# Experts with 96 slots: a weight's chunks first all in one tile shape, then in the other, and the scatter behind the next transposes

## Chip, cores and metric

The kernel runs on one core of a Trainium2 chip. The metric is the device time of one launch in microseconds (us); the text compares medians of several runs, and the profile comes from one execution.

## What is computed

Two decoder layers for 256 tokens of width 1024 (float32). Each layer has a token mixer (SSD, latent attention and a gated unit side by side) and a channel mixer with modulation, residual and layer norm around it. The channel mixer of the second layer is a mixture of 8 experts, and the change lies in it alone:

```python
combine = jnp.sum(jax.nn.one_hot(top_i, N_EXPERTS) * gates[..., None], axis=-2)
for e in range(N_EXPERTS):
    out = out + combine[..., e:e + 1] * swiglu(h, w1[e], w3[e], w2[e])   # silu(h w1) * (h w3), times w2
```

Each token takes two experts. w1 and w3 are 1024 x 2816, w2 is 2816 x 1024.

## The kernel before, in words

The experts are worked off one after the other in 8 places, place 0 to place 7. A place has a fixed number of slots for tokens, `CAPS = [96, 64, 128, 64, 96, 64, 96, 64]`; which expert comes to which place is sorted at run time, and a general loop at the end (`overflow`, skipped here) takes what doesn't fit.

For each place `gather` picks its tokens by matmuls with a one-hot matrix `hot` and transposes them into `st.t`. The hidden width is worked off in three blocks of 1024, 1024 and 768 columns (`BLOCKS = [8, 8, 6]`). `stage1(place, s)` multiplies the tokens by a block of w1 and then of w3 and forms silu(a) * g in `sa`. `turn` transposes `sa`: matmuls with the identity on TensorE (L1093 and L1101; L1086 for 128 slots) into PSUM, from where ScalarE or VectorE copies them. `stage2` multiplies by the block's rows of w2 into `st.po`, which collects all three blocks. After the third block `scatter` copies `po` out of PSUM (L1160, or L1184 and L1185), spreads the rows over the 256 tokens by matmuls with `hott` (L1165, or L1190 and L1191), and VectorE adds them to `yacc` (L1169, L1196). The loop runs stage1 of a block ahead of stage2 of the block before it; in the text, a weight is one block of w1, w3 or w2.

Weights come from DRAM in chunks: `moe_chunk` (L1005) on SP's queue, 280 of them, 35 for each place. A weight of stage1 has four chunks, one of stage2 four, four or three. A chunk lies in one of 11 buffers, taken in turn (6 of `ring`, 5 of `ring2`), and a transfer into a buffer starts when the last instruction that reads the chunk in it is done.

The shape of the matmuls depends on the slots. The stationary operand is the tokens. With 64 slots it has 64 columns, and two matmuls stand side by side in the array (the `wide` shape: L1029 in stage1, L1120 in stage2; 8 records for a chunk). With 96 slots the first 64 go through `wide` and the other 32 through `slim`, four matmuls of 32 columns side by side (L1037 and L1127; 16 records for a chunk, 12 in stage1 of the third block). Both read every chunk. With 128 slots the weights are split into two parts on ScalarE and VectorE (L146, L148) and multiplied by full-width matmuls (L153 to L155).

In the code a weight of a 96-slot place is taken in pairs of chunks: wide 0, wide 1, slim 0, slim 1, then slim 2, slim 3, wide 2, wide 3. The last chunk of a weight with three is slim 2, wide 2.

PSUM buffers come from two pools of four: `acp` (`act_t`: `po`, the transposes, the scatter's and gather's products) and the pool of stage1's sums.

Instructions are not issued in the order of the code. The tile framework fixes each engine's order when the program is built: at each step of its own clock it takes the earliest instruction of the code whose operands it holds to be ready. So a wide pass whose chunk it believes to be still under way is overtaken by a slim pass on a chunk that is there. On the chip the order is then fixed.

Of the kernel before, what the change touches and what calls it, by code (L numbers as in the profile page):

```python
# [52 lines left out]
def tile_decoder(ctx: ExitStack, tc: tile.TileContext, x_in, c_t, c_in, cst, prm, rows, lnrows, gateb, ada, w_in, w_out,  # L53
# [856 lines left out]
    def moe_mixer(x, ad, rs, mp, ring2):  # L910
# [11 lines left out]
        def gather(place):  # L922
            st = state[place] = Ada()
            cap = st.cap = CAPS[place]
            sl, pos = chosen(place, "sl"), chosen(place, "pos")

            hot = mp.tile([P, 2, P], F, tag="hot", name=nm("hot"), bufs=2)
            for i in range(2):
                to, slots = hot[:, i, 0:cap], iota[:, 0:cap]
                if cap == 64:  # L930
                    to = hot[:, i, :].rearrange("p (a s) -> p a s", a=2)
                    slots = iota[:, None, 0:64].to_broadcast([P, 2, 64])
                ins = (pool if place else dve).tensor_scalar(to, slots, pos[:, i, :], sl[:, i, :], op0=OP.is_equal, op1=OP.mult).ins
                if place == 0:
                    mark["hot"] = ins
            st.t = mp.tile([P, KD, P], F, tag="xt", name=nm("xt"), bufs=2)
            scb, shb = ad.sc[:, :, None], ad.sh[:, :, None]

            def put(rows, nq, groups, of, wid):

                g = mp.tile([P, 512], F, tag="gtmp", name=nm("gtmp"))
                act.activation(g[0:rows, 0:nq * P], of[0:rows, 0:nq * P], AF.Copy)
                pt = act_t([P, nq, rows])
                for q in range(nq):
                    pe.transpose(pt[:, q, :], g[0:rows, q * P:q * P + P], ident[0:rows, 0:rows])
                ks, c0 = wid
                pv = pt.rearrange("p q (g s) -> p g q s", g=groups)
                w = rows // groups
                shape = [P, groups, nq, w]
                to = st.t[:, ks, c0:c0 + w].rearrange("p (g q) s -> p g q s", g=groups)  # L950
                bc = [v[:, ks, :].rearrange("p (g q) o -> p g q o", g=groups).to_broadcast(shape) for v in (scb, shb)]
                dve.tensor_tensor(to, pv, bc[0], op=OP.mult)
                dve.tensor_tensor(to, to, bc[1], op=OP.add)

            if cap == P:
                for c in range(2):
                    ps = act_t([P, 512])
                    for i in range(2):
                        pe.matmul(ps, hot[:, i, :], x[:, i, 512 * c:512 * c + 512], start=(i == 0), stop=(i == 1))
                    put(P, 4, 1, ps, (slice(4 * c, 4 * c + 4), 0))  # L960
                st.th = mp.tile([P, KD, P], FR, tag="xhi", name=nm("xth"))
                st.tl = mp.tile([P, KD, P], FR, tag="xlo", name=nm("xtl"))
                for c in range(2):
                    ks = slice(4 * c, 4 * c + 4)
                    act.activation(st.th[:, ks, :], st.t[:, ks, :], AF.Copy)
                    dve.tensor_tensor(st.tl[:, ks, :], st.t[:, ks, :], f32(st.th)[:, ks, :], op=OP.subtract)
            else:
                ps = act_t([P, 512])
                for i in range(2):
                    for c in range(2):  # L970
                        pe.matmul(ps[64 * c:64 * c + 64, :], hot[:, i, 0:64], x[:, i, 512 * c:512 * c + 512],
                                  start=(i == 0), stop=(i == 1), tile_position=(0, 64 * c))
                put(P, 4, 2, ps, (slice(0, KD), 0))
                if cap == 96:
                    ps = act_t([P, 256])
                    for i in range(2):
                        for g in range(4):
                            pe.matmul(ps[32 * g:32 * g + 32, :], hot[:, i, 64:96], x[:, i, 256 * g:256 * g + 256],
                                      start=(i == 0), stop=(i == 1), tile_position=(0, 32 * g))
                    put(P, 2, 4, ps, (slice(0, KD), 64))  # L980
            rows = P if cap == 64 else cap
            st.hott = mp.tile([P, T], F if cap == 64 else FR, tag="hott", name=nm("hott"), bufs=3)
            pt = act_t([P, T])
            for i in range(2):
                pe.transpose(pt[0:rows, i * P:i * P + P], hot[:, i, 0:rows], ident)
            act.activation(st.hott[0:rows, :], pt[0:rows, :], AF.Copy)
# [10 lines left out]
        def moe_chunk(place, n, width=2048):  # L997
# [7 lines left out]
            sp.dma_start(t[:, 0:width], src[:, 0:width])  # L1005
            return t


        def stage1(place, s):
            st = state[place]  # L1010
# [5 lines left out]
            for wsel in range(2):  # L1016
                if st.cap == P:
                    ps = [mmt([P, half]) for _ in range(2)]
                else:
                    ps = mmt([P, half])  # L1020
                    p3 = mmt([P, 256]) if st.cap == 96 else None
                ws = []

                def wide(j):
                    w = ws[j]
                    for k1 in range(2):
                        k = 2 * j + k1
                        for c in range(2):
                            pe.matmul(ps[64 * c:64 * c + 64, :], st.t[:, k, 0:64], w[:, k1, half * c:half * c + half],  # L1029
                                      start=(k == 0), stop=(k == KD - 1), tile_position=(0, 64 * c))  # L1030

                def slim(j):
                    w = ws[j]
                    for k1 in range(2):
                        k = 2 * j + k1
                        for g in range(ng):
                            pe.matmul(p3[32 * g:32 * g + 32, :], st.t[:, k, 64:96], w[:, k1, 256 * g:256 * g + 256],  # L1037
                                      start=(k == 0), stop=(k == KD - 1), tile_position=(0, 32 * g))

                for j in range(4):  # L1040
                    w = moe_chunk(place, 12 * s + 4 * wsel + j, 2 * wd)[:, 0:2 * wd].rearrange("p (k c) -> p k c", k=2)
                    ws.append(w)
                    if st.cap == P:
                        for k1 in range(2):
                            k = 2 * j + k1
                            with ExitStack() as late:
                                if place == 0 and s == 0 and wsel == 0 and k >= EARLY:
                                    late.enter_context(tc.issue_after(mark["hot"]))
                                wh, wl = moe_split(w[:, k1, :], [P, wd])
                            for c in range(2):  # L1050
                                cs = slice(half * c, half * c + half)
                                mm3(ps[c], (st.th[:, k, :], st.tl[:, k, :]), (wh[:, cs], wl[:, cs]), k == 0, k == KD - 1)
                    elif st.cap == 64:
                        wide(j)
                    elif j % 2:
                        for f, jj in ((wide, j - 1), (wide, j), (slim, j - 1), (slim, j)) if j == 1 else (
                                (slim, j - 1), (slim, j), (wide, j - 1), (wide, j)):
                            f(jj)
                out.append(ps if st.cap == P else [ps, p3])
            pa_, pg_ = out  # L1060
            if st.cap == P:
# [44 lines left out]
        def stage2(place, s, th, tl):  # L1106
# [23 lines left out]
            for m in range(nq):  # L1130
                w = moe_chunk(place, 12 * s + 8 + m).rearrange("p (k c) -> p k c", k=2)
                ws.append(w)
                if st.cap == P:
                    whl = [moe_split(w[:, u, :], [P, D]) for u in range(2)]
                    for u, hf in ((0, 0), (0, 1), (1, 0), (1, 1)):
                        wh, wl = whl[u]
                        t = 2 * m + u
                        hs = slice(512 * hf, 512 * hf + 512)
                        mm3(po[hf], (th[:, t, :], tl[:, t, :]), (wh[:, hs], wl[:, hs]), first(t), last(t))
                elif st.cap == 64:  # L1140
                    wide(m)
                elif m % 2 or m == nq - 1:
                    ms = [m - 1, m] if m % 2 else [m]
                    for f in ((wide, slim) if m == 1 else (slim, wide)):
                        for mm in ms:
                            f(mm)

        def scatter(place):
            st = state[place]
# [147 lines left out]
        for place in range(NE):  # L1297
            for s in range(3):
# [4 lines left out]
                sa = stage1(place, s)  # L1303
                if prev is not None:
                    stage2(*prev)
                    if prev[1] == 2:
                        scatter(prev[0])
                prev = (place, s, *turn(place, s, sa))
        stage2(*prev)
        scatter(prev[0])  # L1310
        overflow()
# [210 lines left out]
```

## Time and profile before

| | |
|---|---|
| median of 3 runs | 1257.72 us (1256.67 to 1258.25) |
| the profiled execution | 1257.42 us, its span 1255.6 us |
| TensorE busy | 1170.9 us, 93% of the span |
| VectorE, ScalarE busy | 506.3 us (40%), 384.3 us (31%) |
| experts (stage1 of place 0 to the last stage2) | about 550 us to 1236 us of the span |

Times in rows are microseconds from the span's start. PE is TensorE's matmuls, PEld its loads of the stationary operand, DVE VectorE, ACT ScalarE, POOL GpSimd, SP the queue that issues transfers. A busy TensorE is not TensorE at its peak, since matmuls overlap and their ends are modelled; the starts are what is compared below.

### The profile page before, as it was taken

What the parts mean: (1) busy time and instruction counts of PE and PEld (TensorE: products, weight loads), DVE (VectorE), ACT (ScalarE), POOL (GpSimd) and SP (SyncE); (2) the same over time, 40 slices, a digit from 0 to 9 for tenths busy, and PEclk for the clock granted to TensorE, in tenths of its full rate; (3) what the DMA queues carried; (4) which work ended last, traced back from release to release, by engine and by line L of the source; (5) the groups of instructions that cost most, each with busy time, mean ns of one, the idle gap of its engine ahead of it and who ended that gap; (6) DMA issues with size and microseconds to landing.
All of it is one profiled execution on the core that took longest, in us unless ns stands there. A gap on an engine that the chain in (4) does not pass through costs nothing. (4 is left out here: it accounts for less than half of the span.)

```text
span 1255.6 us, 18705 instructions
## 1 busy us (share of the span) xinstructions
PE 1170.9 (93%) x7667; PEld 704.4 (56%) x7667; DVE 506.3 (40%) x815; ACT 384.3 (31%) x558; POOL 54.5 (4%) x58
## 2 busy tenths in 40 slices
PE   5999979999997999879999999899999999999994
PEld 2877758999986976534433557743334333333331
DVE  2776465777557754521003477630010020300214
ACT  1776435444444754210002457620010010100100
POOL 0100100000000000010000002200000000000001
PEclk9999889999998997989999999999999999999997
DMA  9957646788554475638999999999999999999994
GB/s 378 386 200 295 219 167 227 279 299 332 171 192 167 163 288 198 252 157 312 350 426 408 426 424 367 364 395 349 425 423 371 423 391 426 412 401 375 413 423 163
DMA packets 59592, 402.97 MB, mean 321 GB/s; under 512 B 6751, under 2 KB 7143, under 8 KB 17390
## 3 DMA queue, kind: packets, MB, share of 16 engines
q1 hardware_dynamic: 59358, 401.47, 81.3%
q8 instruction: 62, 1.02, 0.3%
q10 hardware_dynamic: 144, 0.26, 0.1%
q14 instruction: 28, 0.23, 0.0%
HBM read 399.61 MB, written 2.10 MB: 320 GB/s over the span
## 5 line engine op out<-in xcount | busy, mean ns | idle before, releaser
L1029 PE MATMUL mm<-w,xt 128*64 128x512 f32 (+1 forms) x1344 | 288.7, 561 | 0.0
L148 DVE TENSOR_TENSOR wlo<-w,whi 128x1024 fp32r<-128x1024 f32 (+1 forms) x180 | 220.0, 1229 | 111.9 <-ACT whi L146 110.0
L146 ACT ACTIVATE whi<-w 128x1024 fp32r<-128x1024 f32 (+1 forms) x188 | 194.1, 1041 | 177.8 <-PE mm L154 87.8
L1029 PEld LDWEIGHTS mm<-w,xt 128*64 128x64 f32 x1344 | 94.4, 137 | 165.0 <-issue 163.7
L153 PE MATMUL mm<-hhi,whi 128*128 128x256 f32 x608 | 175.5, 290 | 4.8 <-ACT hhi L348 4.8
L154 PE MATMUL mm<-hlo,whi 128*128 128x256 f32 x608 | 174.8, 288 | 0.8 <-DVE hlo L349 0.8
L155 PE MATMUL mm<-hhi,wlo 128*128 128x256 f32 x608 | 173.7, 286 | 0.0
L1072 DVE TENSOR_TENSOR sa<-mm,sa 128x512 f32<-128x512 f32 (+3 forms) x30 | 17.4, 580 | 371.9 <-PE mm L1029 193.0
L1120 PE MATMUL acc<-w,ht 128*64 128x512 f32 x616 | 146.5, 597 | 0.0
L153 PEld LDWEIGHTS mm<-hhi,whi 128*128 128x128 f32 x608 | 118.6, 195 | 9.5 <-ACT hhi L348 6.0
L154 PEld LDWEIGHTS mm<-hlo,whi 128*128 128x128 f32 x608 | 118.6, 195 | 2.4 <-DVE hlo L349 1.8
L155 PEld LDWEIGHTS mm<-hhi,wlo 128*128 128x128 f32 x608 | 118.4, 195 | 0.6 <-issue 0.5
L1120 PEld LDWEIGHTS acc<-w,ht 128*64 128x64 f32 x616 | 43.6, 137 | 81.8 <-issue 80.7
L1071 ACT ACTIVATE sa<-mm 128x512 f32<-128x512 f32 (+3 forms) x30 | 15.2, 507 | 202.6 <-PE mm L1029 116.0
L1095 ACT ACTIVATE ht<-acc 128x512 f32<-128x512 f32 (+1 forms) x21 | 11.8, 561 | 199.2 <-PE acc L1093 199.2
L1037 PE MATMUL mm<-w,xt 128*32 128x256 f32 x1056 | 70.2, 382 | 0.0
L1037 PEld LDWEIGHTS mm<-w,xt 128*32 128x32 f32 x1056 | 34.1, 109 | 44.8 <-issue 24.6
L200 PE MATMUL mm<-w,cs_rep 128*32 128x512 f32 x304 | 41.1, 654 | 9.6 <-DMA w<-in_ada_dram 9.1
L154 PE MATMUL mm<-wlo,xth 128*128 128x512 f32 (+1 forms) x96 | 36.7, 382 | 1.6 <-POOL wlo L148 1.6
L155 PE MATMUL mm<-whi,xtl 128*128 128x512 f32 (+1 forms) x96 | 36.1, 376 | 0.0
L280 POOL TENSOR_TENSOR rs<-rs,mhalf 128x1 f32<-128x1 f32 x14 | 9.1, 652 | 615.9 <-DVE rs L278 615.9
L154 PE MATMUL acc<-wlo,gh 128*128 128x512 f32 x88 | 35.1, 399 | 0.0
(331 smaller groups left out, 1337.9 us busy)
## 6 DMA issues: line engine op xcount, KB each, us to landing
w<-in_moe_dram SPq DMA_DIRECT2D x216, 1024.0 KB, 9.8
w<-in_ada_dram SPq DMA_DIRECT2D x48, 1024.0 KB, 6.7
w<-in_moe_dram SPq DMA_DIRECT2D x64, 768.0 KB, 8.4
w<-in_ffn_dram SPq DMA_DIRECT2D x33, 1024.0 KB, 4.9
w<-in_w_in_dram SPq DMA_DIRECT2D x18, 1024.0 KB, 6.5
w<-in_w_out_dram SPq DMA_DIRECT2D x8, 1024.0 KB, 8.5
lnrow<-in_lnrows_dram SPq DMA_DIRECT2D x5, 1024.0 KB, 4.9
x<-in_x_in_dram SPq DMA_DIRECT2D x2, 512.0 KB
```

What stands on the lines that cost most here:

```text
L146: act.activation(hi, src, AF.Copy)
L148: eng.tensor_tensor(lo, src, f32(hi), op=OP.subtract)
L153: pe.matmul(out_ap, ah, bh, start=start, stop=False)
L154: pe.matmul(out_ap, ah, bl, start=False, stop=False)
L155: pe.matmul(out_ap, al, bh, start=False, stop=stop)
L200: pe.matmul(ps[32 * g:32 * g + 32, :], cs_rep[:, 4 * r + g, :], w[:, g, :], start=(r == 0), stop=(r == 1), tile_position=(0, 32 * g))
L1029: pe.matmul(ps[64 * c:64 * c + 64, :], st.t[:, k, 0:64], w[:, k1, half * c:half * c + half], start=(k == 0), stop=(k == KD - 1), tile_posi ...
L1037: pe.matmul(p3[32 * g:32 * g + 32, :], st.t[:, k, 64:96], w[:, k1, 256 * g:256 * g + 256], start=(k == 0), stop=(k == KD - 1), tile_positi ...
L1071: act.activation(sa[0:rows, :], src[0:rows, :], AF.Silu)
L1072: dve.tensor_tensor(sa[0:rows, :], sg[0:rows, :], sa[0:rows, :], op=OP.mult)
L1095: act.activation(ht, pt, AF.Copy)
L1120: pe.matmul(po[0][64 * c:64 * c + 64, :], th[:, t % nq, c0:c0 + 64], ws[m][:, t % 2, 512 * c:512 * c + 512], start=first(t), stop=last(t), ...
```

## The change

A weight's four chunks go first all through one shape, each as it comes, and after the last of them all four go through the other shape. The next weight of the same place begins with the shape with which the last one ended (`st.turn`), so there is one change of shape in a weight. Stage2 does the same with its four or three chunks. Beside this, in the loop, `turn` of the next place's first block now stands before `scatter` of the place that has just ended, where it stood behind it.

```diff
@@ gather
             cap = st.cap = CAPS[place]
+            st.turn = 1
@@ new function
+        def both(st, wide, slim, j, n):
+            first = (wide, slim)[::st.turn]
+            first[0](j)
+            if j == n - 1:
+                for jj in range(n):
+                    first[1](jj)
+                st.turn = -st.turn
@@ stage1
-                    elif j % 2:
-                        for f, jj in ((wide, j - 1), (wide, j), (slim, j - 1), (slim, j)) if j == 1 else (
-                                (slim, j - 1), (slim, j), (wide, j - 1), (wide, j)):
-                            f(jj)
+                    else:
+                        both(st, wide, slim, j, 4)
@@ stage2
-                elif m % 2 or m == nq - 1:
-                    ms = [m - 1, m] if m % 2 else [m]
-                    for f in ((wide, slim) if m == 1 else (slim, wide)):
-                        for mm in ms:
-                            f(mm)
+                else:
+                    both(st, wide, slim, m, nq)
@@ loop over places and blocks
                     stage2(*prev)
-                    if prev[1] == 2:
-                        scatter(prev[0])
-                prev = (place, s, *turn(place, s, sa))
+                now = (place, s, *turn(place, s, sa))
+                if prev is not None and prev[1] == 2:
+                    scatter(prev[0])
+                prev = now
```

## Rows read from the trace of the kernel before

**Rows 1.** The page: transfer rates in 40 slices; issues by tile.

```profile
GB/s 378 386 200 295 219 167 227 279 299 332 171 192 167 163 288 198 252 157 312 350 426 408 426 424 367 364 395 349 425 423 371 423 391 426 412 401 375 413 423 163
...
w<-in_moe_dram SPq DMA_DIRECT2D x216, 1024.0 KB, 9.8
```

**Rows 2.** Windows by place: stretch, engines' busy us (instructions), clock, DMA share, GB/s.

```profile
550.00:660.00 110.00, 109.99 (x908) 44.12 (x908) 8.29 (x16) 8.61 (x17) 3.29 (x4) 1.00 0.88 345
...
735.00:840.00 105.00, 96.03 (x442) 67.27 (x439) 66.52 (x63) 59.29 (x68) 21.11 (x10) 1.00 0.96 380
...
888.00:1010.00 122.00, 121.08 (x940) 45.65 (x937) 9.96 (x18) 7.45 (x16) 1.80 (x2) 1.00 1.00 410
...
1058.00:1163.00 105.00, 103.26 (x802) 37.16 (x800) 12.88 (x19) 7.03 (x13) 0.00 (x0) 1.00 0.99 398
1163.00:1234.00 71.00, 69.82 (x371) 25.31 (x369) 12.35 (x17) 6.04 (x12) 0.00 (x0) 1.00 0.97 403
```

**Rows 3.** Waits of TensorE from 550 to 1234 us: total, times, longest.

```profile
PE acc L1093 <- DVE sa L1072: 4.0, 5, 1.1
PE acc L154 <- DVE wlo L148: 3.3, 2, 2.0
PE acc L1165 <- ACT o L1160: 2.1, 3, 0.7
...
PE acc L1086 <- DVE yacc L1169: 1.1, 1, 1.1
```

**Rows 4.** Windows at the end of the last place (columns as in rows 2).

```profile
1225.00:1231.00 6.00, 6.00 (x30) 2.01 (x28) 0.00 (x0) 0.00 (x0) 0.00 (x0) 1.00 0.97 404
1231.00:1233.00 2.00, 2.00 (x12) 0.72 (x10) 0.00 (x0) 0.00 (x0) 0.00 (x0) 1.00 0.28 119
```

**Rows 5.** Timeline of TensorE, place 0: start, us, instruction, count.

```profile
583.20 7.09 PE L1029 MATMUL mm<-w,xt 128*64 128x512 f32 x32
590.21 3.66 PE L1037 MATMUL mm<-w,xt 128*32 128x256 f32 x64
593.80 3.65 PE L1029 MATMUL mm<-w,xt 128*64 128x512 f32 x16
```

**Rows 6.** Timeline of TensorE, places 3 and 4.

```profile
888.37 1.89 PE L1029 MATMUL mm<-w,xt 128*64 128x512 f32 x8
890.18 1.07 PE L1037 MATMUL mm<-w,xt 128*32 128x256 f32 x16
891.18 1.94 PE L1029 MATMUL mm<-w,xt 128*64 128x512 f32 x8
893.05 1.93 PE L1037 MATMUL mm<-w,xt 128*32 128x256 f32 x32
...
910.74 5.32 PE L1120 MATMUL acc<-w,ht 128*64 128x512 f32 x24
916.75 1.99 PE L1165 MATMUL acc<-o,hott 64*128 64x512 f32 x8 [0.70 <-ACT o L1160]
918.72 0.66 PE L1093 MATMUL acc<-ident,sa 128*128 128x128 f32 x4
```

**Rows 7.** Timeline of TensorE, place 6.

```profile
1097.63 2.80 PE L1037 MATMUL mm<-w,xt 128*32 128x256 f32 x48
1100.36 1.07 PE L1029 MATMUL mm<-w,xt 128*64 128x512 f32 x2
```

**Rows 8.** Timeline of TensorE, the scatter of place 1.

```profile
737.99 1.99 PE L1165 MATMUL acc<-o,hott 64*128 64x512 f32 x8 [0.70 <-ACT o L1160]
...
741.75 0.66 PE L1086 MATMUL acc<-ident,sa 128*128 128x128 f32 x4 [1.14 <-DVE yacc L1169]
```

**Rows 9.** Timeline of TensorE, the scatter of place 6.

```profile
1187.45 1.08 PE L1029 MATMUL mm<-w,xt 128*64 128x512 f32 x4
1188.46 0.50 PE L1191 MATMUL acc<-ol,hott 96*128 96x512 f32 x1
```

**Rows 10.** Window of place 6 from its gather on (columns as in rows 2).

```profile
1090.00:1163.00 73.00, 71.96 (x568) 26.45 (x569) 10.10 (x15) 4.41 (x9) 0.00 (x0) 1.00 0.97 387
```

## The prediction, made before the changed kernel ran

> **What bounds the kernel now.** I read the page's slices first. From the middle on, where the experts lie, the transfers move 350 to 426 GB/s, far above the first half [rows 1], so both TensorE and the transfers can be the bound. The windows by place tell them apart: TensorE is busy for 109.99 of 110 us in place 0, 121.08 of 122 us around place 4 and 103.26 of 105 us in place 6, at the full granted clock (1.00, the 2.4 GHz level) [rows 2]. The list of its waits for the whole stretch holds no transfer among its larger entries; it names ScalarE and VectorE, with 4.0 us at most in one row [rows 3]. So TensorE's own stream sets the time through place 6, except in place 2, where 96.03 of 105 us are busy and VectorE's splits are among the waits [rows 2, 3].
>
> The transfers are close behind. At their steady rate of about 425 GB/s [rows 1] a chunk of 1024 KB takes 1.0486 MB / 425 = 2.47 us. A place with 64 slots multiplies faster than that, a place with 96 slots slower. So the 11 buffers fill in places 0, 4 and 6 and empty in between. From 1090 to 1163 us the transfers make only 387 GB/s [rows 10]: they wait for buffers, and 73 x (1 - 387/425) = 6.5 us of them are unused. In place 7 they fall to 119 GB/s only at 1231 to 1233 us, two or three microseconds before TensorE has done its last weight [rows 4]. There both end together: what TensorE gains before about 1163 us counts if buffers come free earlier too, and what it gains in place 7 doesn't count.
>
> **Price of a change of shape.** In place 0 a weight goes as written: from the wide pass at 583.20 to the next at 593.80 us lie 32 wide and 64 slim records, 10.60 us, with two changes (wide to slim, slim to wide) [rows 5]. In place 4 the same amount twice runs from 888.37 to 910.74 us, 22.37 us [rows 6], but there the order isn't the written one: after each chunk's wide pass comes its slim pass, and I count 12 changes in these two weights. Two weights at 10.60 us have four changes and take 21.20 us. The difference, 1.17 us for 8 changes, is 0.146 us for one.
>
> The Trainium skill, "TensorEngine Tiling (Array Packing)", Key Properties, says that a change of tiling mode drains TensorE. The trace agrees, at 0.146 us, and the sum below doesn't need the rule.
>
> **How many changes go.** All 27 weights of the three 96-slot places, counted in the timeline of before: place 0 has 18 (two each, as in [rows 5]), place 4 has 32, place 6 has 50, together 100. The edit as written leaves 27. But places 4 and 6 show that the built order isn't the written one: the planner thinks chunks late and lets the other shape overtake [rows 6, 7]. This thought outlives the edit, and the edit feeds it. Written before, a weight needs its third chunk after two wide and two slim passes and its fourth after three slim ones. A chunk takes 7.01/4 = 1.75 us wide and 3.59/4 = 0.90 us slim, from the starts in [rows 5]; that is 5.3 and 6.2 us after the weight's start. In the new order a weight that begins wide wants the fourth after 3 x 1.75 = 5.3 us, and one that begins slim after 2.7 us. Chunks that land 2.47 us apart need 3 x 2.47 = 7.4 us for three after the first, so the planner must see a lead of 1.2 us for the old order, 2.1 us for a weight that begins wide and 4.7 us for one that begins slim. Where it let a wide record in between slim chunk 2 and slim chunk 3, as at 1100.36 us [rows 7], it had less than 1.2 us. There, every new weight is split too, and one split after each chunk has seven changes where the old order, split, had six.
>
> I take: place 0, whose buffers were filled long before, as written, 18 to 9; place 4, 32 to about 37 (its first two weights 12 to 14, those that begin slim split, those that begin wide partly); place 6, 50 to about 58. Together 100 to 104: +4 x 0.146 = **+0.6 us**. Bounds: all as written, 27 changes, -73 x 0.146 = -10.7 us; all split after each chunk, 24 weights with 7 and 3 of three chunks with 5, 183 changes, +12.1 us. I stand nearer to the counts of before, because the cause of the split (the planner's lead) isn't touched.
>
> **The scatter behind the transposes.** After a 64-slot place TensorE waits for ScalarE to copy `po`: three waits, 2.1 us in all, each 0.70 us [rows 3, 6, 8]. Between them, at 918.72 us, stand the next block's transposes, whose input was ready before [rows 6]; moved in front they fill the wait. For the scatters of places 3 and 5 this gives 0.70 us each; 24 wide records from 910.74 us on, at 1.75/8 = 0.219 us, end at 915.99 us, 0.76 us before the scatter's first matmul at 916.75 us; I take 0.75 each, 1.5 us. At place 1 the second half of the transposes also waits 1.14 us for a PSUM buffer that the scatter's adds hold [rows 8]; in front, they find theirs free, since `po` holds one of four and the transposes take two. That is 0.70 + 1.14 = 1.84 us, but place 2 runs behind VectorE's splits (3.3 us of waits in [rows 3]), so I take 1.2 us, with 0 and 1.84 as bounds. After 96- and 128-slot places the planner already fills the scatter's waits with the next block's wide records [rows 9]; the transposes would be one more filler, and the next copy on ScalarE delays the scatter's by as much. I take -0.3 us for places 0 and 2 to 4 together, bounds -1 and +1. Place 6's scatter lies where the transfers bound, nothing. No transfer and no queue entry of SP or POOL moves with it; on ScalarE and VectorE the copies of the transposes stand in front of the scatter's, and behind those waits only the adds to `yacc`, which nobody needs soon. Sum: **-3.0 us**, from +1 to -4.3.
>
> **Buffers held longer.** In the written new order a chunk's buffer comes free only in the second pass: the first of a weight that begins wide after 4 x 1.75 + 0.90 = 7.9 us; before, after two wide and one slim, 4.4 us. With four chunks freed in a burst the transfers start later, but while they are behind there is a queue of them, and a late buffer costs nothing. It costs where they wait for buffers, in places 0, 4 and 6, and it reaches the end only from place 6. There I expect the split order, which frees a chunk right after its two passes as now. I take **+0.3 us**, bounds 0 and +5: 7.9 - 4.4 = 3.5 us for a weight's first chunk, less the queue, in two weights of place 6 that begin wide.
>
> **The sum.** 0.6 - 3.0 + 0.3 = -2.1 us against the profiled execution's 1257.42 us (span 1255.6 us and 1.8 us around it) is 1255.3 us. The median of the runs is 0.3 us above that execution, so I forecast **1255.6 us**.
>
> **Rivals.**
> *The order comes out as written, at least in places 0 and 4.* For it: most of place 4's later weights have two changes each now. Then -9 and -23 changes, -4.7 us, and place 6 stays: with -3.0 us 1250.0 us. With place 6 too it is -10.7 - 3.0 = -13.7 us, 1244 us; against it the split in [rows 7], and that the unused transfer time of place 6 is 6.5 us [rows 10]. Chance 0.25.
> *More changes, not fewer.* Slower: the planner splits every slim-first weight and begins to do so in place 0. Half way to 183 is +41 changes, +6.0 us, with the scatter's -3.0 us 1260.7 us; it decides from about +37 changes (5.5 us), where the total passes +2.5 us. For it: the slim-first weight's need of 4.7 us of lead. Chance 0.13.
> *Buffers freed in bursts starve the transfers of place 6*, so that the end, which the transfers share, comes +5 us later, with no other loss and half of the scatter's gain 1261 us. Chance 0.07.
> *The clock falls.* A weight that begins slim uses four chunks in 3.6 us and would wait up to 4.7 us for its chunks where they aren't ahead. Waits of TensorE of about 1 us left the clock at 1.00 [rows 2, 3]; how it takes several of 4 us in a row no row shows. Four such waits cost 4 x 4.7 = 19 us at worst without any fall of the clock, 1274 us. Against it: the planner orders by a clock that believes transfers late. The Trainium skill, "TensorE: Matmul & The Clock Gate", HAM oscillation, warns of waits for a transfer between groups of matmuls, after which the next group runs at the lower clock; by it each such wait would cost more. Chance 0.03.
> *The scatter alone gains and the changes stay equal*, or both near nothing, is my forecast's own field, 1253 to 1259 us. Chance 0.52.
>
> **Numbers.** 0.2% of 1257.7 us is 2.5 us, about what a measurement of this kernel can tell from no change. Below 1255.2 us lies the first rival and a third of my own field: 0.42. Between, 0.42. Above 1260.2 us the slower rivals, less their mild cases: 0.16. The forecast's own range is 1253 to 1259 us; to hold 8 in 10 it reaches to most of the first rival and of the slower ones: 1249 to 1261.5 us.
>
> **What the profile would show.** The wait L1165 on ScalarE gone for places 1, 3 and 5, the transposes L1093 before L1165. Runs of 64 slim records between wide ones in place 0, one for each weight, and 10.45 us for a weight where rows show 10.60. In places 4 and 6 counts of changes near 37 and 58; if they are near 9, the first rival is right, if place 0 is split, the second. Transfers from 1090 us on below 387 GB/s with a later end of the last chunk would show the third; waits of TensorE for chunks with a clock below 1.00 the fourth. My weakest step is the planner's order: its lead is inferred from few places.

## Result and the profile after

The changed kernel took 1267.05 us in the median (1262.91 to 1268.73), the kernel before, run beside it, 1259.38 us (1256.67 to 1261.77). The ratio is 1.0057, 95% interval 1.0035 to 1.008: slower by some 7 us, where 1255.6 us had been forecast with a range up to 1261.5 us.

The profiled execution took 1265.84 us (span 1264.1 us). Its windows, columns as in [rows 2]; the first five are places 0, 2, 4, 6 and 7, the last three a stretch of place 2:

```profile
551.00:661.00 110.00, 110.00 (x910) 45.41 (x911) 9.11 (x17) 9.63 (x18) 3.29 (x4) 1.00 0.85 343
735.00:840.00 105.00, 95.09 (x433) 66.55 (x430) 67.94 (x63) 59.70 (x69) 18.83 (x9) 0.98 0.94 367
892.00:1014.00 122.00, 120.44 (x899) 43.41 (x895) 9.22 (x16) 7.30 (x14) 1.80 (x2) 1.00 0.98 399
1067.00:1171.00 104.00, 103.18 (x803) 36.10 (x801) 12.89 (x19) 7.04 (x13) 0.00 (x0) 1.00 0.99 402
1171.00:1243.00 72.00, 70.40 (x369) 24.90 (x367) 12.36 (x17) 6.06 (x12) 0.00 (x0) 1.00 0.95 394
...
768.00:772.00 4.00, 1.62 (x9) 1.17 (x8) 4.00 (x3) 1.64 (x3) 2.37 (x1) 1.00 0.76 318
772.00:775.00 3.00, 3.00 (x9) 2.30 (x8) 2.42 (x4) 1.06 (x1) 0.00 (x0) 0.52 0.66 233
775.00:780.00 5.00, 5.00 (x24) 4.06 (x23) 3.45 (x4) 3.19 (x3) 0.00 (x0) 0.95 0.63 226
```

Outside place 2 TensorE is still busy nearly all the time, and none of its waits below is for a transfer, so the transfers are not the new bound; in place 7 they move 394 GB/s where they moved 403 GB/s [rows 2]. Two things are new. In place 2 there are 4 us in which TensorE works for 1.62 us only, and behind them 3 us at a granted clock of 0.52, the 1.2 GHz level. And the list of TensorE's waits (total, times, longest) from 550 to 1243 us has grown:

```profile
PE acc L1101 <- DVE sa L1080: 5.5, 7, 0.9
PE acc L154 <- DVE wlo L148: 4.4, 2, 2.4
PE acc L1170 <- ACT o L1165: 2.1, 3, 0.7
PE mm L154 <- POOL wlo L148: 1.8, 3, 0.7
PE acc L154 <- POOL wlo L148: 1.7, 3, 0.6
PE mm L154 <- DVE wlo L148: 0.7, 1, 0.7
```

Beside [rows 3]: the scatter's wait for ScalarE's copy (L1170, before L1165), which was to go, stands there unchanged, three times 0.7 us. The transposes (L1101, before L1093) wait for VectorE's product 7 times instead of 5. VectorE's splits cost 4.4 us instead of 3.3 us. Only the wait for `yacc`, 1.1 us, is gone.

The timeline of TensorE (start, us, instruction, count) shows how, in places 0, 2, 4 and 5:

```profile
583.40 7.11 PE L1047 MATMUL mm<-w,xt 128*32 128x256 f32 x128
590.44 7.09 PE L1039 MATMUL mm<-w,xt 128*64 128x512 f32 x32
...
768.24 0.62 PE L153 MATMUL acc<-whi,th 128*128 128x512 f32 x2
768.70 0.60 PE L1094 MATMUL acc<-ident,sa 128*128 128x128 f32 x4
771.68 0.50 PE L154 MATMUL acc<-wlo,th 128*128 128x512 f32 x1 [2.38 <-DVE wlo L148]
...
891.54 1.89 PE L1039 MATMUL mm<-w,xt 128*64 128x512 f32 x8
893.35 1.07 PE L1047 MATMUL mm<-w,xt 128*32 128x256 f32 x16
894.36 1.94 PE L1039 MATMUL mm<-w,xt 128*64 128x512 f32 x8
...
912.43 1.94 PE L1039 MATMUL mm<-w,xt 128*64 128x512 f32 x8
914.20 1.89 PE L1128 MATMUL acc<-w,ht 128*64 128x512 f32 x8
916.01 0.66 PE L1101 MATMUL acc<-ident,sa 128*128 128x128 f32 x4
916.51 0.38 PE L1109 MATMUL acc<-ident,sa 128*128 128x128 f32 x2
916.82 3.65 PE L1128 MATMUL acc<-w,ht 128*64 128x512 f32 x16
921.17 1.99 PE L1170 MATMUL acc<-o,hott 64*128 64x512 f32 x8 [0.70 <-ACT o L1165]
...
994.33 13.95 PE L1039 MATMUL mm<-w,xt 128*64 128x512 f32 x64
1009.15 0.66 PE L1101 MATMUL acc<-ident,sa 128*128 128x128 f32 x4 [0.86 <-DVE sa L1080]
```

Place 0 goes as written: 128 slim records of two weights in one run, then wide ones. The first weights of place 4 are split after nearly each chunk. And the transposes don't stand where they are written: at 916.01 us they are drawn in front of the last 16 wide records of place 3, so that nothing is left to fill the scatter's wait; at 1009.15 us in front of the whole last weight of place 4, where their input isn't ready; at 768.70 us in between the matmuls of a weight in place 2.

Where the time went is read best from the length of each place, from its first weight's first matmul to that of the next place (of place 7, to the end of its last weight). Against before, in us (changed kernel and the experiments below, one profile each):

```
             p0     p1     p2     p3     p4     p5     p6     p7
changed    -1.23  +0.34  +3.78  -0.44  +3.36  +1.72  -1.31  +1.20
e1 shapes  -1.23  +0.22  +0.17  -0.03  +2.57  +0.49  -1.23  +0.85
e2 scatter  0.00  -0.22  +5.32  -0.44  -0.08  +0.50  -1.21  +1.16
e3 pinned  -1.23  -0.08  +3.89  -0.44  -4.72  -0.02  -9.28  +4.28
e4 pin.sh. -1.24  -0.48  +1.56   0.00  -4.37  -1.25  -6.22  +3.95
e5 not p2   0.00  -0.21  +0.02  -0.47  -0.07  +0.50  -1.21  +1.16
e6 held     0.00   0.00  +0.13  -0.03  -1.00  +0.01  -2.13  -0.07
e7 p.+held -1.23  -0.48  +1.57  -0.03  -4.01  -1.25  -8.51  +4.28
e8 split   +6.94  +0.45  +1.65   0.00  +3.16  +0.49  -1.92  +0.16
e9 p2 held  0.00   0.00  +1.70  -0.04   0.00  +0.03   0.00  +1.18
e10 halves +9.16  -0.46  +1.58  -0.03  -4.31  -1.25  -6.77  +4.31
e11 all    -1.23  -0.48  +1.54  -0.02  -5.10  -1.25  -8.68  +5.12
```

The changed kernel's places 0 to 7 add up to +7.4 us, as much as the timed difference. What lies before place 0 isn't touched by the change and differs between profiles by up to 13 us (place 0 starts between 548.16 and 561.26 us), so places are compared and not ends. Of place 2's excess in e2, e4 and e7 to e11, 1.5 us is a fall of the clock that came and went without a change of the kernel (last section).

### The profile page after: what moved, and what is told of

Read it like the earlier page. It is cut to its first block, busy times and chain, and to the rows that moved or that the text cites. A ratio compares the mean times of both kernels' runs of the same rounds, so it can differ in the third digit from the quotient of the medians.

```text
span 1264.1 us, 18693 instructions
## 1 busy us (share of the span) xinstructions
PE 1177.2 (93%) x7667; PEld 704.0 (56%) x7667; DVE 508.2 (40%) x815; ACT 384.9 (30%) x558; POOL 54.5 (4%) x58
## 5 line engine op out<-in xcount | busy, mean ns | idle before, releaser
L148 DVE TENSOR_TENSOR wlo<-w,whi 128x1024 fp32r<-128x1024 f32 (+1 forms) x180 | 221.4, 1237 | 110.4 <-ACT whi L146 109.4
L154 PE MATMUL mm<-hlo,whi 128*128 128x256 f32 x608 | 174.8, 288 | 0.8 <-DVE hlo L349 0.8
L154 PEld LDWEIGHTS mm<-hlo,whi 128*128 128x128 f32 x608 | 118.5, 195 | 2.4 <-DVE hlo L349 1.8
L154 PE MATMUL mm<-wlo,xth 128*128 128x512 f32 (+1 forms) x96 | 36.7, 382 | 2.5 <-POOL wlo L148 1.8
L1135 PE MATMUL acc<-w,h 128*32 128x256 f32 x528 | 35.2, 383 | 0.0
```

The source lines that it names most:

```text
L148: eng.tensor_tensor(lo, src, f32(hi), op=OP.subtract)
L154: pe.matmul(out_ap, ah, bl, start=False, stop=False)
L1135: pe.matmul(po[1][32 * g:32 * g + 32, 0:256], tl[:, t % 2, g0:g0 + 32], ws[m][:, t % 2, 256 * g:256 * g + 256], start=first(t), stop=last( ...
```

## Experiments

All ran against the kernel before, in three groups (e1 to e4, e5 to e8, e9 to e11), each group on one chip. The ratio isn't that of the two medians; where the two part, both are given. The first theory was A, that the moved scatter costs and the new shapes lose only because the planner splits them; the rival B, that the shapes themselves are the loss.

**e1, the shapes alone** (the scatter as before):

```diff
-                now = (place, s, *turn(place, s, sa))
-                if prev is not None and prev[1] == 2:
-                    scatter(prev[0])
-                prev = now
+                    if prev[1] == 2:
+                        scatter(prev[0])
+                prev = (place, s, *turn(place, s, sa))
```

> The order of the shapes alone; the scatter stands where it stood. Built, its order has 112 changes of shape against 100 of before (120 in the changed kernel). Theory A (the loss comes from the moved scatter, through place 2 and through transposes that stand in front of a weight and wait): +12 changes at 0.146 us, about +1.8 us, 0 to +4 us over before. Rival B (the loss comes from the shapes, by changes and by buffers held longer): +5 us or more, nearly the changed kernel's time.

Measured: 1259.4 us beside 1260.09 us, ratio 1.0007 (0.998 to 1.0034). The shapes change nothing that can be measured: places 0 and 6 gain 1.2 us each, about what place 4 loses (2.6 us). The interval ends below B's +5 us and holds A's 0 to +4 us.

**e2, the scatter alone** (that edit of the loop, shapes as before).

> The moved scatter alone; the shapes go as before (102 changes). Theory A: place 2 is about 3.6 us longer, and the transposes in front of the last weight of places 4 and 6 cost about 1.6 us each, of which only the first scatters give back 0.4 to 0.7 us each: +4 to +7 us. Rival B: -2 to +1 us, as the prediction had it (-3.0 us for this part).

Measured: 1263.39 us, ratio 1.0029 (1.0005 to 1.0054), slower by 3.6 us (0.6 to 6.8 us); place 2 alone is 5.3 us longer in its profile, 1.5 us of it the clock. This is A's direction, just short of its +4 to +7 us; B's -2 to +1 us only touches the interval's end. A's 1.6 us at each of the last weights of places 4 and 6 isn't there: places 5 and 7 are 0.5 and 1.2 us longer, place 6 is 1.2 us shorter.

**e3, the changed kernel with its second pass queued** behind the last matmul of the first, so that the planner cannot mix them; **e4, the same with the scatter as before** (the lines that note a pass's last matmul in `mark` are left out here and below):

```diff
-                for jj in range(n):
-                    first[1](jj)
+                with tc.issue_after(mark["pass"]):
+                    for jj in range(n):
+                        first[1](jj)
```

> The changed kernel with each weight's second pass queued behind the last matmul of its first pass, so that the order of the shapes comes out as written: 30 changes instead of 120. If a change costs 0.146 us and the buffers do not starve the transfers, 90 x 0.146 = 13 us faster than the changed kernel, so 4 to 7 us faster than before. If held buffers or late chunks bound, TensorE waits for chunks at places 4 and 6 and it is 0 to 10 us slower than before.

> As written, 30 changes, and the scatter where it stood. Theory A with a change at 0.146 us: 70 x 0.146 = 10 us faster than before, and 4 to 7 us faster than the pinned kernel with the moved scatter. Rival B: no better than the pinned kernel with the moved scatter.

Measured: e3 1252.5 us, ratio 0.9914 (0.988 to 0.9947), some 11 us by the ratio and 7.6 us by the medians; e4 1247.91 us, ratio 0.9893 (0.986 to 0.9926), 13.5 us and 12.2 us. Each weight now has one change of shape, 27 as the prediction counts them (30 with the three at the ends of the 96-slot places, which it leaves out), so the edit does what it says, and both beat before by more than the 4 to 7 us and the 10 us expected. Whether e4 beats e3 by A's 4 to 7 us stays open, since the intervals overlap. In the profiles their places add up to nearly the same (-7.6 and -8.1 us, less than the timed gains; the rest isn't located): what e3 loses in place 2 it wins back in place 6. The timeline of e4 in place 4:

```profile
889.00 7.04 PE L1040 MATMUL mm<-w,xt 128*64 128x512 f32 x32
895.96 6.25 PE L1048 MATMUL mm<-w,xt 128*32 128x256 f32 x112
902.95 1.07 PE L1048 MATMUL mm<-w,xt 128*32 128x256 f32 x16 [0.74 <-DMA w<-in_moe_dram]
903.95 7.09 PE L1040 MATMUL mm<-w,xt 128*64 128x512 f32 x32
910.87 5.32 PE L1129 MATMUL acc<-w,ht 128*64 128x512 f32 x24
```

Two weights take 910.87 - 889.00 = 21.87 us, 0.74 us of it a wait for a chunk, where before takes 22.37 us [rows 6] and the changed kernel 914.20 - 891.54 = 22.66 us. What it gains in place 6 it gives back in part in place 7 (-6.2 and +4.0 us). From 1050 us on TensorE now waits for transfers, 2.8 us in place 6 and 2.7 us in place 7:

```profile
PE acc L1129 <- DMA w<-in_moe_dram: 2.3, 5, 0.6
PE mm L1040 <- DMA w<-in_moe_dram: 1.8, 4, 0.5
PE mm L1048 <- DMA w<-in_moe_dram: 1.4, 1, 1.4
```

**e5, e2 without place 2** (`and CAPS[place] != P` in the condition of the moved scatter, the old place otherwise).

> The shapes in the order of before; the transposes are written ahead of the scatter of the place before, except in the place with 128 slots, where the order of before stays. Moved everywhere, the scatter cost 3.3 us (ratio 1.0029), and in that run place 2 was longer by 5.3 us. Theory A, the loss is place 2's (its transposes, planned in front of the last weights of place 1, hold VectorE's splits and TensorE behind them): 0 to +0.8 us, ratio 0.999 to 1.0006. Rival B, the loss lies at each place behind a 96- or 128-slot place, where the transposes now stand directly behind the first weight and wait for VectorE's product (1.1 us each there, three times): +2.5 to +3.5 us, ratio 1.002 to 1.003.

Measured: 1258.35 us beside 1261.35 us, ratio 0.997 (0.9938 to 1.0001). The interval reaches into A's 0.999 to 1.0006 and excludes B's 1.002 to 1.003: the loss of e2 is place 2's. The waits that theory B named are there (L1093 for `sa` 6.6 us, 8 times), but what they cost in places 5 and 7 is made up in places 1, 3 and 6.

**e6, two scatters moved and held**: those of places 3 and 5 only, and the transposes queued behind the last matmul of the weight before.

```diff
                     if prev[1] == 2:
-                        scatter(prev[0])
-                prev = (place, s, *turn(place, s, sa))
+                        if CAPS[place] == 96:
+                            behind = tc.issue_after(mark["s2"])
+                        else:
+                            scatter(prev[0])
+                with behind:
+                    now = (place, s, *turn(place, s, sa))
+                if prev is not None and prev[1] == 2 and CAPS[place] == 96:
+                    scatter(prev[0])
+                prev = now
```

> The shapes in the order of before; only for the scatters of places 3 and 5 are the next transposes written first, and they are queued behind the last matmul of the weight before, so that the planner can't draw them further forward. Theory A, the part would have done what it says if the built order were the written one: transposes fill the wait for ScalarE's copy, the wait L1165 of 0.70 us falls to 0.1 us or less at these two places (one of three is left, at place 1), and the time falls by 0.7 to 0.75 us for each, -1.4 us, ratio 0.9989. Rival B, the wait only changes its place (the next copy on ScalarE stands in front of the scatter's, and the scatter waits for it as long): within 0.3 us, ratio 1.000, and the waits L1165 stay near 0.7 us.

Measured: 1259.09 us, ratio 0.9962 (0.9932 to 0.9993). The interval holds A's 0.9989 and ends just below B's 1.000. One of three waits L1165 is left, and place 4 is 1.00 us shorter. The timeline there:

```profile
917.11 5.32 PE L1120 MATMUL acc<-w,ht 128*64 128x512 f32 x24
922.36 0.66 PE L1093 MATMUL acc<-ident,sa 128*128 128x128 f32 x4
922.86 0.38 PE L1101 MATMUL acc<-ident,sa 128*128 128x128 f32 x2
923.17 1.99 PE L1165 MATMUL acc<-o,hott 64*128 64x512 f32 x8
```

This is the order that the change writes and didn't get: the scatter starts 0.81 us behind the transposes' start, without a wait. Theory A holds for these two scatters. Place 6 is even 2.13 us shorter, but only some 1.0 us of this is waits: it also has two wide starts fewer (0.86 us; the table under e8 says what they are), which nobody planned and which e2 and e5 have too.

**e7, e4 with the two scatters of e6.**

> The second pass of each 96-slot weight queued behind the first, which gave 30 changes of shape and ratio 0.9893, and with it the two scatters of places 3 and 5 with the next transposes queued in front. Theory A: both gains add up where TensorE is the bound, -0.7 us for place 3; at place 5 the same 0.7 us, but the last weights wait for transfers by 2 us and more, so that it doesn't reach the end: ratio 0.9885 to 0.989 of before. Rival B, the end is set by the transfers alone, whose buffers come free no earlier: no more than with the shapes alone, ratio 0.9893 to 0.990.

Measured: 1250.19 us, ratio 0.9896 (0.9854 to 0.9937). Not to be told from e4; between A and B it decides nothing. Place 6 is 2.3 us shorter than in e4, and place 7 hardly longer (0.3 us).

**e8, every chunk split**: wide and slim by turns, each pass of a weight queued behind the one before (the lines of `both` that go are left out).

```diff
+            with tc.issue_after(mark["pass"]) if j else ExitStack():
+                wide(j)
+            with tc.issue_after(mark["pass"]):
+                slim(j)
```

> The price of a change of shape, by itself: every 96-slot chunk multiplied wide and then slim at once, each pass queued behind the one before, which gives 210 changes where before has 100; the scatter as before. Theory A, the time follows the number of changes: 110 more at 0.146 us are +16.1 us, at the 0.17 us of the run with 30 changes (12.2 us for 70) +18.9 us; ratio 1.0128 to 1.015. A buffer comes free right after its two passes, so that the transfers wait for nothing. Rival B, the changes cost little by themselves and the gain of the queued order came from weights that no longer wait for chunks: 0 to +4 us, ratio 1.000 to 1.003.

Measured: 1269.05 us beside 1261.35 us, 7.7 us by the medians; ratio 1.0034 (1.0007 to 1.006), 0.9 to 7.6 us. That is far below A's +16 us, and the interval reaches into B's 0 to +4 us; so the total doesn't follow the number of changes. Yet in place 0 the price is as A has it, 8.17 us more than in the changed kernel for 55 more changes, 0.149 us each, and in place 4 it is 0.137 us (7.53 us more than in e4 for 55); but in place 6, with 17 changes more than before, the place is 1.9 us shorter. So before loses something there that isn't a change of shape. Counting the starts of matmuls in the records showed what:

```
         changes in place   starts of wide/slim groups    length us
          0   4   6         0        4        6           0      4       6
before   16  28  46      130/128  146/128  148/134      87.74   99.43  105.06
changed   8  42  54      130/128  148/132  146/132      86.51  102.79  103.75
e4        8   8   8      130/128  142/128  142/128      86.51   95.06   98.84
e8       63  63  63      130/128  142/128  142/128      94.68  102.59  103.15
e10       8   8   8      152/128  142/128  142/128      96.90   95.13   98.30
```

(Changes are counted here between a place's first matmul and the next place's.) The two halves of the array work side by side: wide records start two at a time every 0.43 us, slim ones four at a time every 0.22 us. A matmul has two records. The instructions are the same in all kernels, but where the planner cuts a run behind an odd matmul, that matmul has no partner, and its two records start one behind the other, 0.43 us each, as the single wide matmul at 1100.36 us in [rows 7] does (two records, 1.07 us to the end of the second). Each odd piece costs one start more than it would in pairs, and a cut leaves two such pieces. Before has 4 such extra starts in place 4, and 6 wide and 6 slim ones in place 6.

**e9, the scatter of place 1 alone, held** as in e6 (the transposes of place 2 queued behind the last matmul of place 1).

> The shapes in the order of before; only for the scatter of place 1 are the next transposes (those of the 128-slot place) written first, and they are queued behind the last matmul of place 1. Moved freely, this scatter made place 2 longer by 3.8 us in the changed kernel and 5.3 us with the scatter alone. Theory A, the planner's freedom is what costs (it draws the second transposes between the matmuls of a weight, where they wait for VectorE's split): held in their written place, place 2 loses nothing, and the 1.14 us wait L1086 for yacc and the 0.70 us wait L1165 of place 1 go: place 2 shorter by 1.2 to 1.8 us, the whole by 1 to 2 us, ratio 0.9985 to 0.999. Rival B, the adds to yacc that now stand behind the copies of the transposes delay VectorE's splits in place 2 in any order: place 2 longer by 2 us or more, ratio 1.0015 to 1.003.

Measured: 1259.99 us beside 1260.28 us, ratio 1.0002 (0.9978 to 1.0025). The time alone decides nothing, since the interval reaches into both A's and B's numbers. In the profile the 3.8 us are gone, so the planner's freedom was what cost, against B; but A's gain isn't there either. The waits L1165 and L1086 are gone, and place 2 is 0.9 us ahead 50 us into it; then its weights come in another order, with a wait of 0.81 us for GpSimd's split that before doesn't have there, and at 810 us it is 0.1 us behind. The rest of its +1.70 us is the clock, see the end.

**e10, the halves apart**: e4, but in the first two weights of place 0 all wide matmuls of one half of the array first, then all of the other.

```diff
-                    for k1 in range(2):
...
+                    order = [(2 * j + k1, c) for k1 in range(2) for c in range(2)]
+                    if place == 0 and s == 0:
+                        order = [(k, c) for c in range(2) for k in range(8)] if j == 3 else []
+                    for k, c in order:
```

> On top of the queued passes (30 changes of shape): in place 0, in the first two weights, the wide matmuls go all of one half of the array first and then all of the other, instead of the halves by turns. Theory A, wide matmuls on the two halves run two at a time in 0.43 us, and one that has no partner beside it takes the same 0.43 us alone, so that a run cut behind an odd matmul costs 0.43 us beyond the change of shape: each of these weights has 16 such pairs, and the two weights take up to 2 x 16 x 0.43 = 13.7 us more; place 0 is longer by 11 to 14 us. Rival B, the pairing is only how the records are written and the array's columns set the time: place 0 is the same within 0.5 us.

Measured: 1262.77 us, ratio 1.0023 (1.0005 to 1.0042). The timeline of the first weights in place 0:

```profile
561.26 12.29 PE L1041 MATMUL mm<-w,xt 128*64 128x512 f32 x32
573.48 7.11 PE L1049 MATMUL mm<-w,xt 128*32 128x256 f32 x128
580.52 12.29 PE L1041 MATMUL mm<-w,xt 128*64 128x512 f32 x34
```

32 wide records take 12.29 us where by turns they take 7.09 us (the changed kernel at 590.44 us). Place 0 is 96.90 - 86.51 = 10.39 us longer than in e4: 22 more starts x 0.429 = 9.4 us, and of the other 0.95 us a wait of 0.79 us for VectorE's product. A bit under the 11 us of A, since 22 of the 32 pairs came apart; B falls.

**e11, e7 with the scatter of place 1 too.**

> The second pass of each 96-slot weight queued behind the first, and the scatters of places 1, 3 and 5 with the next transposes queued in front. Theory A: the queued passes gave 0.9893, and with two scatters 0.9896, since the last weights wait for transfers; what place 2 gives (1.2 to 1.8 us) comes before the places where buffers are full, so a part of it reaches the end: ratio 0.988 to 0.9895. Rival B, the end is set by transfers alone: 0.9893 to 0.9905, with longer waits for transfers in place 7 (above the 7.2 us of the run with the two scatters).

Measured: 1253.75 us (1245.05 to 1260.01), ratio 0.9944 (0.9913 to 0.9975). Neither theory's number: the interval lies above A's 0.988 to 0.9895 and B's 0.9893 to 0.9905. No better than e4 or e7 and, with overlapping intervals, not shown to be worse; its profile is the shortest of all (span 1244.1 us), so why the timed gain is smaller stays open. Of the versions tried, e4 has the lowest ratio.

## Why the prediction was wrong

The measured 1267.05 us lies above the range, and above the numbers of the rival of more changes (1260.7 us) and of the one of the buffers (1261 us).

**The bound: right.** TensorE's stream sets the time through place 6 and the transfers are close behind it; e4 shows how close, where 5.5 us of waits for chunks appear in places 6 and 7.

**The price of a change of shape, 0.146 us: right.** e8 gives 0.149 us in place 0 and 0.137 us in place 4.

**The number of changes: mis-sized.** The step was 100 to 104, with the planner's split left as it is. Counted as there, by weight, the changed kernel has 11, 47 and 59, together 117. Place 0 and place 6 are nearly as forecast (9 and 58); place 4 has 47 instead of 37, since weights that begin wide are split there as well. With that the +0.6 us become 17 x 0.146 = +2.5 us. The rival of more changes had this mechanism, but began at +37 changes; there were +17.

**What the step left out: the cuts inside a run.** In place 4 the changed kernel is 3.36 us longer. Two more wide starts (0.86 us) and four more slim ones (0.86 us) are half of it; the time around the transposes is 0.22 us shorter, which leaves 1.86 us for the 14 changes of the count above (0.133 us each). In place 6 eight more changes cost 1.1 us; two wide and two slim starts fewer (1.29 us), a wait of 0.73 us less (for VectorE's product, at 1151.82 us in before) and 0.48 us less around the transposes give more than that back. The price of the cuts was in the trace of before, about 10 x 0.43 + 6 x 0.216 = 5.6 us in places 4 and 6, and the prediction did not see it, because it counted records in runs and not their starts. The Trainium skill, "TensorEngine Tiling (Array Packing)", Key Properties, says that different tiles multiply in parallel; e10 agrees, with 12.29 us against 7.09 us.

**The scatter behind the transposes, -3.0 us with bounds +1 and -4.3: this step failed.** Alone it costs 3.6 us (e2). It took the written order for the built one, though the same text had shown, for the shapes, that the planner doesn't keep it. Free of the scatter, the planner drew the transposes further forward: past the place where they would have filled the wait. In places 3 and 5 the mechanism was right and is worth 0.75 us as worked out, if the order is held (e6: 0.9 us of waits gone in place 4, the place 1.0 us shorter). At place 1, with the transposes held, 0.9 us of the 1.2 us are there at first, but they are lost again to another order of the weights behind (e9). In the built order place 2 loses 3.8 us: a wait of 2.38 us for VectorE's split, where before waits 0.60 us for one of GpSimd's, and behind it the fall of the clock, 3 us at 0.52 for 1.4 us lost. Why the split was late stands in VectorE's timeline, first before, then the changed kernel:

```profile
766.76 1.23 DVE L148 TENSOR_TENSOR wlo<-w,whi 128x1024 fp32r<-128x1024 f32 x1 [0.17 <-DMA w<-in_moe_dram]
...
767.74 0.69 DVE L1073 TENSOR_TENSOR sa<-mm,sa 128x512 f32<-128x512 f32 x1 [1.18 <-PE mm L155]
```

On VectorE the planner now put the product that the transposes need (L1073) in front of this split. VectorE stands idle for 1.18 us until TensorE is done with its input, and the split that before began at 766.76 us begins at 768.35 us, just behind one of GpSimd's (L148 runs there too), and takes 3.28 us instead of 1.23 us (last section).

With place 2 left as before, the loss isn't there (e5), so it is place 2's. The allowance for places 0 and 2 to 4, -0.3 us from -1 to +1, was about right: -0.2, -0.4 and +0.5 us in places 1, 3 and 5 (e2). For place 6's scatter the prediction had nothing; place 7 is 1.2 us longer, 0.86 us of it a wait of the transposes for VectorE's product, but it is as much longer in e9, which leaves this scatter alone, so a price for it isn't shown.

**Buffers held longer, +0.3 us: no sign of it.** TensorE waits for no chunk in the changed kernel, whose order in places 4 and 6 is split as before's is. In the written order of e4 it does, 5.5 us from 1050 us on; whether because buffers come free in bursts or because TensorE is faster wasn't separated.

**The rivals.** The order as written was given 1250 us, or 1244 us with place 6. e3 has that order with the scatter as the change moves it, 7.6 us (medians) to 11 us (ratio) faster than before; e4 without it, 12.2 to 13.5 us. So the 13.7 us given for it were of the right size, but partly by luck: the price was put together from 73 changes and 3.0 us of the scatter, where the runs have 70 changes (with the ends of places), about 5.6 us of cuts, waits for chunks that take some of it back, and no gain of the scatter. The planner kept it from happening. The fall of the clock, given 0.03 because TensorE would wait for chunks, came by another way: one wait, for VectorE, in place 2. The Trainium skill, "TensorE: Matmul & The Clock Gate", HAM oscillation, says that a group of matmuls behind a wait for a transfer runs at the lower clock; the trace agrees for a wait for VectorE, with 0.52 behind 2.38 us, here and in e2 and e3, the other two profiles with this wait.

The two parts give 0.9 us (e1) and 3.6 us (e2), 4.5 us, where the changed kernel lost some 7 us (1.0035 to 1.008). In the profiles the places give 1.8 us (e1) and 3.5 us (e2, without the clock's 1.5 us), where the changed kernel has 7.4 us. A part of the gap is that the edits act on each other through the planner: by weight the changed kernel has 117 changes of shape, e1 109 and e2 102, so 6 more than the two add up to, 0.9 us. The rest stays open; place 5 is 1.72 us longer with both, 0.5 us with either.

## What to carry to other kernels

Where a planner sets the order, an edit of the written order is a hint: read from the trace how far it kept to the old one, and queue what must stay together behind its neighbour, else moving one block frees others to go where they wait. Where matmuls share the array, count starts and not records: a cut behind an odd matmul leaves two without a partner, here two wide starts or 0.86 us, nearly six times a change of shape. And work moved in front to fill a wait has to be held there, just before the wait.

## What the runs showed of the hardware

Place 2 has, in every kernel here, a wait of 2.0 us for VectorE's split, between 801 and 824 us by kernel (the longest in the row L154 of [rows 3]). Behind it the granted clock stayed at 1.00 in the profiles of before, the changed kernel, e1, e3, e5 and e6, and fell in the seven others, of which four (e4, e7, e8, e10) have the same order of TensorE's instructions in this place as before; that costs 1.5 us. In e4, columns as in [rows 2]:

```profile
802.00:808.00 6.00, 4.83 (x15) 3.84 (x16) 4.41 (x5) 2.42 (x3) 0.04 (x1) 0.72 0.91 344
```

So a wait of this size can lower the clock or not, and a place's length may differ by 1.5 us for no reason in the kernel; what decides it wasn't found.

In the changed kernel VectorE's split at 768.35 us took 3.28 us, where the same form takes 1.23 us, while GpSimd made another split. The first line is VectorE's timeline, the second GpSimd's:

```profile
768.35 3.28 DVE L148 TENSOR_TENSOR wlo<-w,whi 128x1024 fp32r<-128x1024 f32 x1
...
768.18 2.37 POOL L148 TENSOR_TENSOR wlo<-w,whi 128x1024 fp32r<-128x1024 f32 x1 [6.86 <-ACT whi L146]
```

GpSimd's split ended at 770.55 us, 2.20 us behind VectorE's start; with VectorE's own 1.23 us that makes 3.43 us, about the 3.28 us seen, as if VectorE had stood still until GpSimd was done. The Trainium skill, "SBUF — State Buffer", Terms, says that the two share a pair of ports that the one holds for a whole instruction while the other is blocked; the trace agrees within 0.2 us. A split of before that began 1.05 us ahead of the end of GpSimd's (769.56 and 770.61 us) took 2.13 us, again about the rest of that one and 1.23 us.
